# Encoder trunk in f32r halves: raw output weights also in uncomputed columns of the result, pairs in chunks 1 to 5, sums of y in chunk 0

## The chip, the cores and the metric

The kernel runs on one core of a Trainium2 chip. The metric is the device time of one execution in microseconds, as a median of three runs.

## The reference

One layer of an encoder over 256 tokens of width 4096, in float32. The stream is normalised, one input projection feeds a gated short convolution (2048 channels) and windowed attention (16 heads), both gated; their outputs, concatenated to y, pass through one output projection and a second layer norm:

```python
h = layer_norm(x, emb_ln_g, emb_ln_b)
p = h @ w_in                                    # 256 x 4096 times 4096 x 13312
y_conv = c_b * centred_short_conv(c_c * c_h, conv_w) * silu(c_z)
y_attn = banded_window_attention(a_q, a_k, a_v, sink) * silu(a_z)
y = concatenate([y_conv, y_attn]) @ w_out       # 256 x 4096 times 4096 x 4096
out = layer_norm(2 ** 0.25 * h + y, ln_g, ln_b)
```

## The kernel before

**Halves.** Each f32 operand is split into a hi part (rounded to f32r) and a lo part (the rest), and each product is three matmuls: hi x hi, hi x lo, lo x hi (L210 to L212 and L841 to L843). The weights come as raw f32 from memory. ACT copies them to `whi` (`split_hi`, L170), DVE subtracts to get `wlo` (`split_lo`, L174); three buffers of each. `xT` holds both halves of the left operand for all 32 k-tiles, first of h, later of y.

**Steps.** All weight work is one list of steps. A whole step ("s") is four k-tiles of 512 output columns, 128x2048 raw values, 1 MB, 24 matmuls of 512 columns. A pair ("S") is two k-tiles by a scheme of Strassen's kind (`mm_pair`): seven products of half size instead of eight, 21 matmuls of 256 columns, 0.5 MB raw. For a pair DVE first makes three further sums of its raw blocks (`sums`, L154 to L156, below called the adds), and the left operand has sums and differences of its own, kept in the tile `SC` (`x_sums`). `pair_copy` and `pair_sums` put the products together at the end of a chunk.

**The output projection** goes over nine chunks of output columns: seven of 512 (0 to 6) and two of 256 (7, 8). `OUT_ORDERS` gives each chunk's steps. The result collects in `R` (128 x 2 x 4096: two row tiles), chunk by chunk from column 0 on. A chunk's end (`end_out`) adds the accumulators to R and takes the statistics (L860), `end_out2` multiplies by ln_g (L864). The residual of a chunk (`res_load`) is five transfers of 256 KB each: rows of the two embedding parameters and of ln_g, broadcast to all partitions, into `gb`, and x into `xc`; `residual` (L823, L825) makes alpha times h from them. `gb` and `xc` have one buffer each. `finish_...` make the second norm at the end; `rows_load` and `rows_split` bring ln_g and ln_b to it in 15 small transfers.

**Order.** It is written by hand: at step j PE gets the matmuls of j, ACT the hi copy of j+3, then come what is due by `at`, the loads, DVE's adds of step j+4 and its lo subtraction of j+3. Each engine and SP's queue work in that order. A raw load goes to the buffer that was used longest ago: with three buffers (w0 to w2), the load of j+6 waits for the lo subtraction of j+3.

```python
while nxt < len(steps) and nxt <= j + 7:
    (u, _), bs = w_bufs(nxt)
    if u > j + (2 if len(bs) > N_W else 3):
        break
```

N_IN is the first step of the output projection. `open_p2` opens the pool of R, gb, xc and the tiles of the end at step N_IN+5, in memory that the convolution's tiles held.

Of the kernel before, what the change touches and what calls it, by code (L numbers as in the profile page):

```python
# [8 lines left out]
F32 = mybir.dt.float32  # L9
# [35 lines left out]
ORDERS = {0: "s" * 8, NP: "sSsSSsSsSSs"}  # L45
OUT = 100
OP = 4
OUT_ORDERS = ["s" * 8, "ssSsSsSsSs"] + ["sSsSssSsSs"] * 5 + ["", ""]
N_W = 3


# [43 lines left out]
def encoder_kernel(ctx: ExitStack, tc: tile.TileContext, x, emb_g, emb_b, wi, ws, conv_w, sink, wo, ln_g, ln_b, out):  # L95
# [43 lines left out]
    def loads(j):

# [8 lines left out]
    def sums(j):  # L149

        if j >= len(steps) or not is_pair(j):
            return
        r = raw[j].rearrange("p (b w) -> p b w", w=HW)
        nc.vector.tensor_tensor(r[:, 4:6, :], r[:, 1:3, :], r[:, 0:1, :].to_broadcast([P, 2, HW]), op=ALU.add)  # L154
        nc.vector.tensor_tensor(r[:, 6, :], r[:, 5, :], r[:, 1, :], op=ALU.add)
        nc.vector.tensor_tensor(r[:, 7, :], r[:, 6, :], r[:, 3, :], op=ALU.add)  # L156
# [432 lines left out]
    def sum_tile(ci):  # L589

        if ci >= OUT:
            return R[:, :, (ci - OUT) * W:(ci - OUT + 1) * W]
        kind = IN_ORDER[ci]
        if kind >= C_AZ:
            return pa.tile([P, 2, W], F32, name="z")
        if kind >= C_Q:
            return pa.tile([P, 2, W], F32, name="q")
        name = "ug" if kind < C_CC or C_CH <= kind < C_CZ else "tm"
        if pc is not None:
            return pc.tile([P, 2, W], F32, name=name)  # L600
# [90 lines left out]
    def at(j, fn, *a):  # L691
        later.setdefault(j, []).append((fn, a))
# [109 lines left out]
    def res_load(n):  # L802
# [202 lines left out]
```

## Time and profile before

| | us |
|---|---|
| median of three runs (1569.02 to 1569.75) | 1569.3 |
| the profiled execution | 1571.03 |
| its span | 1569.3 |

| engine | busy us | share of the span |
|---|---|---|
| PE | 1528.5 | 97% |
| PE weight loads | 1328.2 | 85% |
| DVE | 1298.2 | 83% |
| ACT | 759.7 | 48% |

The mean granted clock of TensorE is 0.991 of full speed. A share of busy time is a mean over the whole span; what stops PE in one stage is read from that stage's waits and timeline. "PE busy" counts a matmul until its modelled end, so the distance from one matmul's start to the next one's tells its cost.

### The profile page before, as it was taken

Reading aid. Unit: us, or ns where it says so; the run is one execution under the profiler, and the core shown is the slowest. Engines: PE = TensorE matmul, PEld = TensorE weight load, DVE = VectorE, ACT = ScalarE, POOL = GpSimd, SP = SyncE. Lnnn points to the kernel's source line nnn. Section 1 sums busy time; section 2 is a strip of 40 time slices with the busy share of each in tenths; the row PEclk is TensorE's granted clock in tenths of the full one; section 3 lists DMA queues with packets and bytes.
Section 4 is the critical chain, followed back from the end, with each engine's and each line's share of the span. In section 5 each row is a group of like instructions: output and inputs, shape, how many; then the busy total and the mean of one; then the engine's idle time right before and its main releaser. Section 6 shows DMA issues by size and latency. Waiting matters only on the chain.

```text
span 1569.3 us, 21272 instructions
## 1 busy us (share of the span) xinstructions
PE 1528.5 (97%) x8694; PEld 1328.2 (85%) x8694; DVE 1298.2 (83%) x1494; ACT 759.7 (48%) x642; POOL 1.3 (0%) x7
## 2 busy tenths in 40 slices
PE   7999999999999999999999999999999899899997
PEld 4888888888888888888888888888888787787896
DVE  8678789888888889888888888888887889678786
ACT  4544556556564654544444454454554334333341
POOL 0000000000000000000000000000000000000000
PEclk9999999999999999999999999999999999999998
DMA  7545554546445457555555655565557564665563
GB/s 296 210 143 197 199 203 158 189 167 209 178 181 188 158 183 256 204 200 191 210 201 183 220 187 203 192 210 203 198 194 262 178 232 166 224 209 216 205 244 128
DMA packets 65889, 312.99 MB, mean 199 GB/s; under 512 B 7968, under 2 KB 11520, under 8 KB 41728
## 3 DMA queue, kind: packets, MB, share of 16 engines
q1 hardware_dynamic: 65216, 310.06, 55.5%
q8 instruction: 68, 1.11, 0.3%
q10 hardware_dynamic: 576, 1.57, 0.3%
q14 instruction: 29, 0.24, 0.0%
HBM read 303.66 MB, written 7.86 MB: 199 GB/s over the span
## 4 chain that ended last, share of the span: by engine, by line
PE 78%; DVE 11%; DMA 5%; ACT 3%; issue 3%; SPq 1%; DVEq 0%; ACTq 0%
PE acc L210 14%; PE acc L212 14%; PE acc L211 14%; DVE wlo L174 5%; PE pacc L235 4%; PE pacc L234 4%; PE pacc L236 4%; PE acc L842 3%; DMA w<-in_ws 3%; PE acc L843 3%; PE acc L841 3%; PE acc L235 3%; PE acc L234 3%; PE acc L236 3%; ACT whi L170 2%
## 5 line engine op out<-in xcount | busy, mean ns | idle before, releaser
L170 ACT ACTIVATE whi<-w 128x2048 fp32r<-128x2048 f32 (+1 forms) x353 | 640.4, 1816 | 730.2 <-PE acc L212 288.8
L174 DVE TENSOR_TENSOR wlo<-w,whi 128x2048 fp32r<-128x2048 f32 (+1 forms) x353 | 759.5, 2161 | 163.3 <-ACT whi L170 161.4
L210 PE MATMUL acc<-whi,xT 128*128 128x512 f32 x1072 | 424.3, 396 | 0.0
L212 PE MATMUL acc<-whi,xT 128*128 128x512 f32 x1072 | 419.8, 392 | 0.0
L211 PE MATMUL acc<-wlo,xT 128*128 128x512 f32 x1072 | 417.8, 390 | 0.7 <-DVE wlo L174 0.7
L212 PEld LDWEIGHTS acc<-whi,xT 128*128 128x128 f32 x1072 | 201.3, 188 | 46.8
L211 PEld LDWEIGHTS acc<-wlo,xT 128*128 128x128 f32 x1072 | 201.4, 188 | 41.2 <-DVE wlo L174 1.0
L210 PEld LDWEIGHTS acc<-whi,xT 128*128 128x128 f32 x1072 | 201.5, 188 | 37.9
L842 PE MATMUL acc<-wlo,xT 128*128 128x512 f32 (+1 forms) x464 | 172.5, 372 | 18.8 <-DVE wlo L174 18.8
L843 PE MATMUL acc<-whi,xT 128*128 128x512 f32 (+1 forms) x464 | 172.3, 371 | 0.0
L841 PE MATMUL acc<-whi,xT 128*128 128x512 f32 (+1 forms) x464 | 171.5, 370 | 0.0
L154 DVE TENSOR_TENSOR w<-w 128x512 f32<-128x512 f32 x168 | 114.9, 684 | 46.7 <-DMA w<-in_ws 46.6
L842 PEld LDWEIGHTS acc<-wlo,xT 128*128 128x128 f32 x464 | 88.9, 192 | 36.1 <-DVE wlo L174 21.5
L235 PE MATMUL pacc<-wlo,SC 128*128 128x256 f32 x360 | 101.4, 282 | 0.0
L841 PEld LDWEIGHTS acc<-whi,xT 128*128 128x128 f32 x464 | 89.0, 192 | 14.5 <-issue 0.4
L843 PEld LDWEIGHTS acc<-whi,xT 128*128 128x128 f32 x464 | 89.0, 192 | 14.4
L236 PE MATMUL pacc<-whi,SC 128*128 128x256 f32 x360 | 101.1, 281 | 0.0
L234 PE MATMUL pacc<-whi,SC 128*128 128x256 f32 x360 | 101.1, 281 | 0.0
L235 PE MATMUL acc<-wlo,xT 128*128 128x256 f32 x336 | 93.8, 279 | 0.0
L234 PE MATMUL acc<-whi,xT 128*128 128x256 f32 x336 | 93.7, 279 | 0.0
L236 PE MATMUL acc<-whi,xT 128*128 128x256 f32 x336 | 93.6, 279 | 0.0
L234 PE MATMUL pacc<-whi,xT 128*128 128x256 f32 x312 | 89.1, 286 | 0.0
(205 smaller groups left out, 1812.7 us busy)
## 6 DMA issues: line engine op xcount, KB each, us to landing
w<-in_wi SPq DMA_DIRECT2D x134, 1024.0 KB
w<-in_ws SPq DMA_DIRECT2D x168, 512.0 KB
w<-in_wo SPq DMA_DIRECT2D x52, 1024.0 KB
yl<-yd SPq DMA_DIRECT2D x7, 512.0 KB
xc<-in_x SPq DMA_DIRECT2D x14, 256.0 KB
x<-in_x SPq DMA_DIRECT2D x6, 512.0 KB
first<-in_wi SPq DMA_DIRECT2D x2, 1024.0 KB
yd<-zT SPq DMA_DIRECT2D x16, 128.0 KB
```

The source lines that it names most:

```text
L154: nc.vector.tensor_tensor(r[:, 4:6, :], r[:, 1:3, :], r[:, 0:1, :].to_broadcast([P, 2, HW]), op=ALU.add)
L170: nc.scalar.activation(part(j, wh[j]), part(j, raw[j]), AF.Copy)
L174: nc.vector.tensor_tensor(part(j, wl[j]), part(j, raw.pop(j)), part(j, wh[j]).bitcast(F32), op=ALU.subtract)
L210: nc.tensor.matmul(a, xh, hk, start=(first and k == 0), stop=False)
L211: nc.tensor.matmul(a, xh, lk, start=False, stop=False)
L212: nc.tensor.matmul(a, xl, hk, start=False, stop=(last and k == PK - 1))
L234: nc.tensor.matmul(o, ah, hi[:, w, :], start=(opens and p == 0), stop=False)
L235: nc.tensor.matmul(o, ah, lo[:, w, :], start=False, stop=False)
L236: nc.tensor.matmul(o, al, hi[:, w, :], start=False, stop=(closes and last))
L841: nc.tensor.matmul(o, yh, hk, start=first, stop=False)
L842: nc.tensor.matmul(o, yh, lk, start=False, stop=False)
L843: nc.tensor.matmul(o, yl, hk, start=False, stop=last)
```

## The change

It has four parts. (1) While chunks 0 to 6 run, raw weights are also loaded into columns of R that are not computed yet: from step N_IN+6 on into R0 and R1 (columns 2048 to 4095 of the two row tiles, one raw buffer each, until the chunk that writes them nears its end), then into R2 (columns 3072 to 4095 of both row tiles, one buffer), so that there are five, then four buffers; with more than three, a load waits for a lo subtraction that already stands ahead of it in the order. (2) The pairs are in chunks 1 to 5 (four each); chunk 6 has whole steps, as chunk 0. (3) The sums of y, `x_sums` for four pairs, run at the steps 1, 2, 4 and 5 of the projection instead of 6, 8, 9 and 10; their tile takes over the memory of the input projection's SC, so it need not wait for the pool of R. (4) `end_out2` and the next `res_load` move from the end of a chunk to step 0 of the next, behind its lo subtraction; the residual is made at step 4 of a chunk. Tiles that shared R's last columns move, and t5 shrinks to 72 columns to make room.

```diff
-OUT_ORDERS = ["s" * 8, "ssSsSsSsSs"] + ["sSsSssSsSs"] * 5 + ["", ""]
+OUT_ORDERS = ["s" * 8] + ["sSsSsSsSss"] * 5 + ["s" * 8, "", ""]
...
+    in_R = [(steps.index(("opair", OUT + 4, OP - 1)) + 1, "R0"), (steps.index(("opair", OUT + 4, OP - 1)) + 1, "R1"),
+            (steps.index(("out", OUT + 6, NPC - 1)), "R2")]
 
     def w_bufs(j):
 
         bs = [(wpool, f"w{k}") for k in range(N_W)] + (extra if j < N_IN else [])
-        return min((user.get(b, -1), k) for k, b in enumerate(bs)), bs
+        if j >= N_IN and R is not None:
+            late = j > in_R[0][0]
+            bs += [(None, name) for last, name in in_R if j <= last and late == (name == "R2")]
+        last_user = lambda b: max(u for c, u in user.items() if c == b or b[1] == "R2" and c[0] is None) if (
+            b in user or b[1] == "R2") else -1
+        return min((last_user(b), k) for k, b in enumerate(bs)), bs
...
-            to = raw[j] = pool.tile([P, PIECE], F32, name=name, bufs=1)
-        if is_pair(j):
+            if pool is None:
+                to = raw[j] = {"R0": R[:, 0, D // 2:D], "R1": R[:, 1, D // 2:D], "R2": R[:, :, 3 * D // 4:D]}[name]
+            else:
+                to = raw[j] = pool.tile([P, PIECE], F32, name=name, bufs=1)
...
-    psc = phs.enter_context(tc.tile_pool(name="psc", bufs=1))
+    psc = ctx.enter_context(tc.tile_pool(name="psc", bufs=1))
     SC = psc.tile([P, NP, 2, 3, HT], F32R, name="SC")
-    extra.append((psc, "w6"))
+    pw = phs.enter_context(tc.tile_pool(name="pw", bufs=1))
+    extra.append((pw, "w6"))
...
+    def y_sums(k):
+        nonlocal SC
+        if k == 0:
+            t = psc.tile([P, NP * 2 * 3, HT], F32R, name="SCy", tag="SC")
+            SC = t[:, 0:OP * 8, :].rearrange("p (k h s) t -> p k h s t", k=OP, h=2)
+        x_sums(k, pc.tile([P, 4 * S], F32, name="xs", tag="tm"))
+
     for k in range(OP):
-        at(N_IN + (6, 8, 9, 10)[k], lambda k: x_sums(k, R[:, 1, D - 4 * S:D]), k)
+        at(N_IN + (1, 2, 4, 5)[k], y_sums, k)
+    ends = []
...
-            if t == (0 if n == ncs - 1 else 2 if not np_ and n else (7, 5, 4)[min(n, 2)]):
+            if t == 0 and n:
+                for a in ends:
+                    end_out2(*a)
+                ends = []
+                if n < ncs - 1:
+                    res_load(n)
+            if t == (0 if n == ncs - 1 else 2 if n == ncs - 2 else 4 if n else 7):
                 residual(n)
...
         if n < ncs - 1:
-            for i in range(2):
-                end_out2(n, i, end_out(n, i))
-            if n + 1 < ncs - 1:
-                res_load(n + 1)
+            ends = [(n, i, end_out(n, i)) for i in range(2)]
```

Three places where the rows show it. On SP's queue around the end of chunk 1 (w0 to w2 are the raw buffers; `in_ws` holds pairs, `in_wo` whole steps; gb and xc are the residual's loads), before:

```order
L135 DMA w2_10624<-in_ws 128x1024
L137 DMA w0_10655<-in_wo 128x2048
L137 DMA w1_10691<-in_wo 128x2048
L813 DMA gb_10704<-in_emb_g_row 128x512
L814 DMA gb_10704<-in_emb_b_row 128x512
L815 DMA gb_10704<-in_ln_g 128x512
L817 DMA xc_10705<-in_x 128x512 x2
L135 DMA w2_10739<-in_ws 128x1024
L137 DMA w0_10768<-in_wo 128x2048
```

and now (R is a raw buffer in the result's tile):

```order
L151 DMA R_10285<-in_ws 128x1024
L153 DMA R_10285<-in_wo 128x2048
L151 DMA w1_10664<-in_ws 128x1024
L153 DMA w2_10694<-in_wo 128x2048
L151 DMA w0_10733<-in_ws 128x1024
L841 DMA gb_10739<-in_emb_g_row 128x512
L842 DMA gb_10739<-in_emb_b_row 128x512
L843 DMA gb_10739<-in_ln_g 128x512
L845 DMA xc_10740<-in_x 128x512 x2
L153 DMA R_10285<-in_wo 128x2048 x2
```

Ahead of the residual's loads the queue now holds the pair and the whole step that came behind them; two whole steps into R come behind them.

On DVE at the end of chunk 0 and the start of chunk 1, before (L859 and L860 are `end_out`, L864 the products with ln_g, L578 to L446 a piece of the sums of y, L154 to L156 the adds of a pair):

```order
L859 SCALAR_TENSOR_TENSOR R_10249<-xc_10262,acc_10034 128x512
L860 BN_STATS s20_10250<-R_10249 128x6
L864 TENSOR_TENSOR R_10249<-R_10249,gb_10261 128x512
L859 SCALAR_TENSOR_TENSOR R_10249<-xc_10262,acc_10038 128x512
L860 BN_STATS s21_10251<-R_10249 128x6
L864 TENSOR_TENSOR R_10249<-R_10249,gb_10261 128x512
L578 TENSOR_TENSOR R_10249<-xT_86 128x512
L583 TENSOR_TENSOR R_10249<-R_10249 128x128 x4
L446 TENSOR_TENSOR SC_10253<-R_10249,SC_10253 128x512
L154 TENSOR_TENSOR w2_10305<-w2_10305 128x512
L155 TENSOR_TENSOR w2_10305<-w2_10305 128x256
L156 TENSOR_TENSOR w2_10305<-w2_10305 128x256
```

and now (L887 and L888 are `end_out`, L201 the lo subtraction, L892 the products, L178 to L180 the adds):

```order
L887 SCALAR_TENSOR_TENSOR R_10285<-xc_10297,acc_10037 128x512
L888 BN_STATS s20_10286<-R_10285 128x6
L887 SCALAR_TENSOR_TENSOR R_10285<-xc_10297,acc_10041 128x512
L888 BN_STATS s21_10287<-R_10285 128x6
L201 TENSOR_TENSOR wlo_10411<-R_10285,whi_10407 128x1792
L892 TENSOR_TENSOR R_10285<-R_10285,gb_10296 128x512 x2
L178 TENSOR_TENSOR w1_10336<-w1_10336 128x512
L179 TENSOR_TENSOR w1_10336<-w1_10336 128x256
L180 TENSOR_TENSOR w1_10336<-w1_10336 128x256
L201 TENSOR_TENSOR wlo_10451<-R_10285,whi_10445 128x2048
```

The products stand behind the lo subtraction of the step three ahead, and the sums of y are gone from here.

They stand on DVE in chunk 0, at its steps 4 and 5. Before (L174 lo subtraction, L686 the lo half of y, L781 and L783 the memsets of t5):

```order
L174 TENSOR_TENSOR wlo_10181<-w2_10069,whi_10173 128x2048
L686 TENSOR_TENSOR xT_86<-yl_10101,xT_86 128x4x256
L174 TENSOR_TENSOR wlo_10214<-w0_10103,whi_10207 128x2048
L686 TENSOR_TENSOR xT_86<-t0_9467,xT_86 128x2x256
L686 TENSOR_TENSOR xT_86<-t1_9468,xT_86 128x2x256
L781 MEMSET t5_10255 128x256
L783 MEMSET t5_10255 128x2x2 x3
L174 TENSOR_TENSOR wlo_10270<-w1_10145,whi_10240 128x2048
```

and now (L607 to L475 are a piece of the sums of y, L715 the lo half of y):

```order
L201 TENSOR_TENSOR wlo_10201<-w2_10072,whi_10193 128x2048
L715 TENSOR_TENSOR xT_86<-yl_10104,xT_86 128x4x256
L607 TENSOR_TENSOR xs_10232<-xT_86 128x512
L612 TENSOR_TENSOR xs_10232<-xs_10232 128x128 x4
L475 TENSOR_TENSOR SCy_10106<-xs_10232,SCy_10106 128x512
L201 TENSOR_TENSOR wlo_10242<-w0_10115,whi_10227 128x2048
L715 TENSOR_TENSOR xT_86<-t0_9470,xT_86 128x2x256
L715 TENSOR_TENSOR xT_86<-t1_9471,xT_86 128x2x256
L607 TENSOR_TENSOR xs_10272<-xT_86 128x512
L612 TENSOR_TENSOR xs_10272<-xs_10272 128x128 x4
L475 TENSOR_TENSOR SCy_10106<-xs_10272,SCy_10106 128x512
```

Each piece comes ahead of the lo subtraction of its step.

## Rows read from the trace of the kernel before

**Rows 1.** The waits between engines from 1150 us to the end (who waited <- for whom: us in total, times, longest us).

```profile
DVE w L154 <- DMA w<-in_ws: 44.3, 15, 8.8
...
PE acc L842 <- DVE wlo L174: 18.8, 7, 5.2
```

**Rows 2.** The timeline of PE in the output projection: its matmuls that stood idle before they began (start us, duration us, engine, line, operation, [idle us before <- releaser]). These eight are all of them from the first to the last output matmul.

```profile
1240.26 0.58 PE L842 MATMUL acc<-wlo,xT 128*128 128x512 f32 x1 [3.92 <-DVE wlo L174]
...
1252.01 0.50 PE L842 MATMUL acc<-wlo,xT 128*128 128x512 f32 x1 [1.94 <-DVE wlo L174]
...
1297.32 0.51 PE L842 MATMUL acc<-wlo,xT 128*128 128x512 f32 x1 [2.19 <-DVE wlo L174]
...
1347.27 0.80 PE L842 MATMUL acc<-wlo,xT 128*128 128x512 f32 x1 [5.24 <-DVE wlo L174]
...
1394.95 0.50 PE L842 MATMUL acc<-wlo,xT 128*128 128x512 f32 x1 [1.83 <-DVE wlo L174]
...
1440.53 0.51 PE L842 MATMUL acc<-wlo,xT 128*128 128x512 f32 x1 [2.46 <-DVE wlo L174]
...
1486.43 0.51 PE L842 MATMUL acc<-wlo,xT 128*128 128x512 f32 x1 [1.17 <-DVE wlo L174]
...
1538.74 0.38 PE L842 MATMUL acc<-w,xT 128*128 128x256 f32 x1 [0.77 <-DVE w L174]
```

**Rows 3.** Stretches of the span (us from its start: length; busy us and count of PE, PEld, DVE, ACT, POOL; granted TensorE clock as a share of full speed; busy share of the DMA engines; GB/s). The first is the whole projection, the others are the stretches just behind four of the gaps.

```profile
1178.00:1555.00 377.00, 357.48 (x1961) 308.30 (x1959) 295.54 (x338) 147.62 (x95) 0.00 (x0) 0.98 0.58 206
1240.00:1244.00 4.00, 3.75 (x9) 2.97 (x10) 3.23 (x8) 2.11 (x2) 0.00 (x0) 0.57 0.48 164
1298.00:1302.00 4.00, 4.00 (x13) 3.10 (x11) 2.62 (x4) 0.73 (x1) 0.00 (x0) 0.57 0.72 262
1346.00:1354.00 8.00, 6.73 (x17) 5.31 (x18) 6.59 (x6) 2.68 (x2) 0.00 (x0) 0.57 0.54 197
1440.00:1446.00 6.00, 5.47 (x17) 4.33 (x18) 4.71 (x6) 1.94 (x2) 0.00 (x0) 0.72 0.64 232
```

**Rows 4.** The chain that ended last, in order of time, around the end of chunk 1 (start us, us, what).

```profile
1283.21 0.33 SPq L813
...
1285.55 7.81 DMA w<-in_ws
...
1293.45 0.70 DVE w L154
...
1294.98 2.30 DVE wlo L174
...
1297.32 0.51 PE acc L842
```

**Rows 5.** The same chain at the ends of chunks 2 and 5: the load behind the residual's loads.

```profile
1333.93 9.38 DMA w<-in_ws
...
1475.99 6.48 DMA w<-in_ws
```

**Rows 6.** The timeline of PE around one whole step of four k-tiles and one pair (start us, duration us): the first matmul of the step, of the pair, and of the pair behind it. The same two sorts of step stand in the projection.

```profile
1143.22 0.40 PE L210 MATMUL acc<-whi,xT 128*128 128x512 f32 x1
...
1148.73 0.28 PE L234 MATMUL pacc<-whi,xT 128*128 128x256 f32 x1
...
1151.20 0.28 PE L234 MATMUL pacc<-whi,xT 128*128 128x256 f32 x1
```

**Rows 7.** The timeline of DVE in chunk 1 (start us, us, engine, line, operation, count, [idle before <- releaser]). The length of a piece of work is the start of the next row's work less its own start.

```profile
1240.12 0.68 DVE L578 TENSOR_TENSOR R<-xT 128x512 f32<-128x512 f32 x1
...
1243.16 2.02 DVE L174 TENSOR_TENSOR wlo<-w,whi 128x1792 fp32r<-128x1792 f32 x1
...
1261.31 0.74 DVE L823 SCALAR_TENSOR_TENSOR xc<-xc,musd,gb 128x512 f32<-128x512 f32 x1
...
1264.21 2.29 DVE L174 TENSOR_TENSOR wlo<-w,whi 128x2048 fp32r<-128x2048 f32 x1
...
1272.30 0.41 DVE L614 TENSOR_TENSOR R<-R,pacc 128x256 f32<-128x256 f32 x1
...
1275.27 0.69 DVE L154 TENSOR_TENSOR w<-w 128x512 f32<-128x512 f32 x1
...
1276.79 2.28 DVE L174 TENSOR_TENSOR wlo<-w,whi 128x2048 fp32r<-128x2048 f32 x1
1278.99 0.68 DVE L857 TENSOR_TENSOR R<-acc,R 128x512 f32<-128x512 f32 x1
...
1283.11 4.22 DVE L174 TENSOR_TENSOR wlo<-w,whi 128x1792 fp32r<-128x1792 f32 x2
```

**Rows 8.** ACT's hi copies in the projection, by shape (xcount | busy us, mean ns | idle before, releasers): 128x2048 for a whole step, 128x1792 for a pair.

```profile
L170 ACT ACTIVATE whi<-w 128x2048 fp32r<-128x2048 f32 x49 | 93.9, 1915 | 109.3 <-PE acc L843 78.0 <-issue 11.6 <-PE pacc L236 8.6
L170 ACT ACTIVATE whi<-w 128x1792 fp32r<-128x1792 f32 x24 | 40.9, 1702 | 92.9 <-PE acc L843 48.6 <-DVE w L156 36.6 <-PE pacc L236 4.2
```

**Rows 9.** The timeline of DVE in chunk 0: the lo subtractions for the steps 7 and 8 from the start of the projection, each of which began when ACT's hi copy was done.

```profile
1208.12 2.29 DVE L174 TENSOR_TENSOR wlo<-w,whi 128x2048 fp32r<-128x2048 f32 x1 [2.06 <-ACT whi L170]
...
1213.66 2.29 DVE L174 TENSOR_TENSOR wlo<-w,whi 128x2048 fp32r<-128x2048 f32 x1 [1.50 <-ACT whi L170]
```

**Rows 10.** The stretch from the first of chunk 2's residual loads to the landing of the pair's load behind them (columns as in rows 3).

```profile
1283.20:1293.40 10.20, 10.20 (x57) 8.80 (x56) 4.12 (x2) 2.18 (x2) 0.00 (x0) 1.00 0.83 256
```

**Rows 11.** The timeline of SP's queue: the 15 small transfers of `rows_split` in chunk 2 (start us, us until the last was issued).

```profile
1319.16 11.55 SPq L800 DMA_DIRECT2D rows<-R  x15
```

More of the change, by code (lines that the diff above doesn't have):

```diff
@@ L117, in encoder_kernel @@
     raw, wh, wl = {}, {}, {}
-    psc = pc = None
+    psc = pw = pc = R = None
     extra = []
     user = {}
+    in_R = [(steps.index(("opair", OUT + 4, OP - 1)) + 1, "R0"), (steps.index(("opair", OUT + 4, OP - 1)) + 1, "R1"),
+            (steps.index(("out", OUT + 6, NPC - 1)), "R2")]
     def w_bufs(j):
         bs = [(wpool, f"w{k}") for k in range(N_W)] + (extra if j < N_IN else [])
-        return min((user.get(b, -1), k) for k, b in enumerate(bs)), bs
+        if j >= N_IN and R is not None:
[4 more added lines that the diff above has]
+        return min((last_user(b), k) for k, b in enumerate(bs)), bs
     def load(j, to=None):
@@ L132, in load @@
             user[bs[k]] = j
-            to = raw[j] = pool.tile([P, PIECE], F32, name=name, bufs=1)
-        if is_pair(j):
+            if pool is None:
+                to = raw[j] = {"R0": R[:, 0, D // 2:D], "R1": R[:, 1, D // 2:D], "R2": R[:, :, 3 * D // 4:D]}[name]
+            else:
+                to = raw[j] = pool.tile([P, PIECE], F32, name=name, bufs=1)
+        src = wi[IN_PIECES.index((a, b))] if kind == "in" else wo[OUT_PIECES.index((a, b))] if kind == "out" else None
+        if len(to.shape) == 3:
+            if is_pair(j):
+                nc.sync.dma_start(out=to[:, 0, :], in_=ws[ALL_PAIRS.index((a, b))])
+            else:
+                nc.sync.dma_start(out=to, in_=src.rearrange("p (i n) -> p i n", i=2))
+        elif is_pair(j):
             nc.sync.dma_start(out=to[:, 0:4 * HW], in_=ws[ALL_PAIRS.index((a, b))])
         else:
-            nc.sync.dma_start(out=to, in_=wi[IN_PIECES.index((a, b))] if kind == "in" else wo[OUT_PIECES.index((a, b))])
+            nc.sync.dma_start(out=to, in_=src)
     def loads(j):
@@ L152, in sums @@
             return
[L153 to L156, printed above, removed]
+        if len(raw[j].shape) == 3:
+            r0, r1 = (raw[j][:, i, :].rearrange("p (b w) -> p b w", w=HW) for i in range(2))
+            r = lambda k: (r1 if k >= 4 else r0)[:, k % 4, :]
+            s01 = r1[:, 0:2, :]
+            b12, b22 = r0[:, 0:1, :], r0[:, 1:3, :]
+        else:
+            t = raw[j].rearrange("p (b w) -> p b w", w=HW)
+            r = lambda k: t[:, k, :]
+            s01, b12, b22 = t[:, 4:6, :], t[:, 0:1, :], t[:, 1:3, :]
+        nc.vector.tensor_tensor(s01, b22, b12.to_broadcast([P, 2, HW]), op=ALU.add)
+        nc.vector.tensor_tensor(r(6), r(5), r(1), op=ALU.add)
+        nc.vector.tensor_tensor(r(7), r(6), r(3), op=ALU.add)
     def part(j, t):
+        if len(raw[j].shape) == 3:
+            return t if len(t.shape) == 3 else t.rearrange("p (i n) -> p i n", i=2)
         return t[:, HW:] if is_pair(j) else t
@@ L173, in split_lo @@
         wl[j] = half_tile(j, "wlo")
-        nc.vector.tensor_tensor(part(j, wl[j]), part(j, raw.pop(j)), part(j, wh[j]).bitcast(F32), op=ALU.subtract)
+        nc.vector.tensor_tensor(part(j, wl[j]), part(j, raw[j]), part(j, wh[j]).bitcast(F32), op=ALU.subtract)
+        raw.pop(j)
     def split(j):
@@ L601, in sum_tile @@
         if name == "tm":
-            st_["cu"] = psc.tile([P, 2, 2, W], F32, name="w6", bufs=1)
+            st_["cu"] = pw.tile([P, 2, 2, W], F32, name="w6", bufs=1)
         return st_["cu"][:, 1 if name == "ug" else 0, :, :]
@@ L737, in encoder_kernel @@
         if j == z0 + 6:
-            extra.insert(0, (psc, "w6"))
+            extra.insert(0, (pw, "w6"))
         mm_pair(j) if kind == "pair" else mm(j)
@@ L761, in encoder_kernel @@
     res = {}
-    p2 = R = st2 = ms2 = rows = t5 = lhs5 = None
+    p2 = st2 = ms2 = rows = t5 = lhs5 = None
     RB = [(0, 0), (0, 1), (0, 2), (32, 0), (32, 1), (32, 2), (64, 0), (64, 1)]
@@ L770, in open_p2 @@
     def open_p2():
-        nonlocal p2, R, st2, ms2, rows, t5, lhs5, SC
+        nonlocal p2, R, st2, ms2, rows, t5, lhs5
         ph.close()
@@ L777, in open_p2 @@
         ms2 = p2.tile([P, 2, 4], F32, name="ms2")
-        SC = p2.tile([P, OP, 2, 4, HT], F32R, name="SC")
         rows = p2.tile([P, 3 * W], F32R, name="rows")
-        t5 = p2.tile([P, 2, P], F32, name="t5")
+        t5 = p2.tile([P, 2, 72], F32, name="t5")
         nc.vector.memset(t5, 0.0)
@@ L789, in rows_load @@
         for k, src in enumerate((ln_g, ln_b)):
-            w = lnw[k] = R[0:KT, k, D - 4 * P:D - 3 * P]
+            w = lnw[k] = R[0:KT, k, 3 * W:3 * W + P]
             nc.sync.dma_start(out=w, in_=src.rearrange("(a b) -> a b", b=P))
@@ L794, in rows_split @@
         for k, (slots_h, slot_l) in enumerate((((0, 1), 2), ((3,), 4))):
-            w, hl = lnw[k], R[0:KT, k, D - 3 * P:D - P].bitcast(F32R).rearrange("p (a b) -> p a b", a=2)
+            w, hl = lnw[k], R[0:KT, k, 3 * W + P:3 * W + 3 * P].bitcast(F32R).rearrange("p (a b) -> p a b", a=2)
             nc.vector.tensor_copy(hl[:, 0, :], w)
@@ L809, in res_load @@
         else:
-            z = p2.tile([P, OP * 2 * 4, HT], F32, name="z", tag="SC").rearrange("p a b -> p (a b)")
+            z = psc.tile([P, NP * 2 * 3, HT], F32, name="z", tag="SC").rearrange("p a b -> p (a b)")
             gb = z[:, 0:3 * w].rearrange("p (a b) -> p a b", a=3)
@@ L881, in finish_tr @@
         tp = ps_att.tile([P, P], F32, name="att")
-        nc.tensor.transpose(tp, t5[:, i, :], ident)
+        nc.tensor.transpose(tp[0:72, :], t5[:, i, :], ident)
         nc.scalar.activation(lhs5[0:69, i, :], tp[0:69, :], AF.Copy)
```

## The prediction

> **What bounds the kernel now.** I read the page first, then the waits of the last quarter, PE's timeline there, the granted clock, the chain and DVE's timeline. The change touches nothing ahead of the output projection, so only its 377 us count. The page has PE busy for 97% of the span, and in the projection it is busy for 357.5 of 377 us [rows 3]: the bound is PE, with gaps. The gaps are eight, each in front of the second matmul of a step, which needs the step's lo half from DVE: 3.92 + 1.94 + 2.19 + 5.24 + 1.83 + 2.46 + 1.17 + 0.77 = 19.5 us [rows 2]. Behind the gaps of 3.92, 2.19, 5.24 and 2.46 us the granted clock stands at its lower level (1.2 instead of 2.4 GHz) for some us. The loss is the share below 1 times the length: 0.43 x 4 + 0.43 x 4 + 0.43 x 8 + 0.28 x 6 = 8.6 us [rows 3]; the whole projection's 0.98 of 377 us says that little is lost elsewhere. After the gaps of 1.94, 1.83 and 1.17 us it stayed high. Gaps and clock together: 28.1 us.
>
> Why is DVE late? It waited 44.3 us for pair loads [rows 1], and since it works in order, a pair's adds that wait for their load hold up the lo subtraction queued behind them, which PE needs sooner. The worst loads stand behind the residual's five loads, at a chunk's end. There the chain goes: products with ln_g done, first residual load issued at 1283.21, the pair's load issued at 1285.55 and landed 7.81 us later, adds at 1293.45, lo at 1294.98, PE at 1297.32 [rows 4]. At other chunk ends that load took 9.38 and 6.48 us [rows 5].
>
> **The parts of the change, with t for a step of a chunk and E(t) for the time PE ends it.** A whole step takes PE 5.51 us, a pair 2.47 [rows 6].
>
> *Pairs in five chunks.* Four pairs (9.9 us) become two whole steps (11.0): +1.1 us of PE time, on the path.
>
> *Raw buffers in R.* With three buffers a load waited for the lo subtraction three steps ahead of it; with five (chunks 1 to 4) it waits for the one five steps ahead, with four (chunk 5) four. In a paired chunk two steps are 8.0 us, about what the late pair loads took. SP's rows show it: seven steps are loaded ahead of the residual's loads instead of six, and no pair load follows them in these chunks. Bytes are the same (four loads of half a MB for two of one), and the DMA engines were busy for 0.58 of the stage [rows 3].
>
> Does DVE then keep up? Work per paired chunk [rows 7]: six whole lo at 2.2 (1276.79 to 1278.99), four pair lo at 2.0, four adds at 1.5 [rows 4], 3.0 for the pairs' sums with the residual (1272.30 to 1275.27), 2.9 for the residual (1261.31 to 1264.21), 4.1 for the chunk's end (1278.99 to 1283.11): 37.3 us of PE's 42.9. Counted from E(0): E(1) 2.5, E(2) 8.0, E(3) 10.5, E(4) 16.0, E(5) 18.4, E(6) 23.9, E(7) 26.4. A hi copy starts when PE has freed its buffer and takes 1.9 us, for a pair 1.7 [rows 8]. So lo(3) ends at 3.7, the moved products at 5.1, adds(5) at 6.6, lo(4) at 8.8, due at 10.5. Later hi(7) ends at 17.7, lo(7) at 19.7, the residual at 22.6, lo(8) at 24.8, due at 26.4. The margin is 1.6 us at both places and larger elsewhere: no gap in chunks 2 to 4. The old end-of-chunk gaps go; what is late next is the pair load in chunk 5. Its four buffers leave the pair of t = 7 behind the residual's loads: products at 5.1, plus 10.2 us from first residual issue to adds [rows 4], is 15.3, where lo(5) ended at 11.7. Adds to 16.8, lo(6) to 19.0, due at 18.4: +0.6 us.
>
> The DVE and ACT operations that read R have no row; their shapes are those of the w buffers, so I take the same durations. Bounds: nothing either way, since where R is an operand a row is no slower (0.68 us for 128x512 at 1240.12 [rows 7], 0.70 for the same size in w [rows 4]).
>
> `rows_split` in chunk 2 still puts 15 small transfers on SP, 11.6 us [rows 11]. Two raw loads stand behind them; counting on from the chunk's end they land some 11 to 13 us into chunk 3, wanted at 10.5 to 11.7 with 2 us to spare before PE notices: 0, at most 3.
>
> *Products and residual loads one step later.* The two products (a third of 4.1, 1.4 us) leave the chunk's end and go behind lo(3). At the very end this also puts the last lo ahead of them, so the 0.77 us gap goes. Queued behind the moved loads on SP are the loads for t = 8 and 9, wanted 10 us after.
>
> *Sums of y in chunk 0.* Four pieces of 3.0 us each (1240.12 to 1243.16) leave chunks 0 and 1, where they made the gaps of 3.92 and 1.94 us, for t = 1, 2, 4 and 5 of chunk 0. There DVE waited 2.06 and 1.50 us for ACT ahead of lo(7) and lo(8) [rows 9], so the first three cost only DVE's spare time. In the old run lo(7) began at 1208.12 and lo(8) at 1213.66, with 1.8 us of other work between. Now the sums at t = 4 make lo(7) end at about 1212.8 (1208.1, three ACT copies and one DVE subtraction of together 2.5, then 2.2), the last sums end at 1217.3, adds(9) at 1219, lo(8) at 1221.2. PE ended step 5 at 1213.66 - 1.92 = 1211.7, so it ends step 7 at 1222.7: 1.5 us to spare.
>
> *What is late next: the start of chunk 1.* R can be used only once the last sums of y are done, because its pool opens then, and SP puts chunk 0's residual loads ahead of the first R load. Issue at 1217.3 plus 10.2 gives 1227.5 for the pair of step 11. DVE, idle from 1223, then has adds(11) to 1229.0 and lo(10) to 1231.2, due at 1230.7: 0.5 late. Residual 2.9 and chunk end without products 2.7: 1236.9. lo(11) to 1238.9, due at 1236.7: 2.2 late. Products 1.4, adds(13) 1.5, lo(12) 2.2: 1244.0, due at 1241.4: 2.6 late. Together 5.3 us of gaps, and one spell at the lower clock, 1.7 us, as after the gaps of 2.19 and 2.46: 7.0 us. If the load lands 4 us sooner nearly all of it goes; if 3 us later, and with two spells, it is 12.
>
> Here a rule of the Trainium skill bears (DMA: Bandwidth & Descriptors, Queues, rings and completion order): each DMA engine takes the descriptors of one queue in ring order, so loads issued behind the pair's would not delay it. The trace does not quite agree: until that pair landed 10.2 us x 256 GB/s = 2.6 MB had moved [rows 10], 0.8 MB more than residual and pair hold, so some of the later load went too. By the rule the 10.2 us stand and the sum is 1550; by sharing, the half MB more behind the pair now adds 2 us and the sum is 1552.
>
> *The sum.* 1569.3 - 28.1 + 1.1 + 7.0 + 0.6 = 1549.9 us of span. The profiled execution took 1571.03 us with a span of 1569.3, so 1.7 us lie around the span; the median of the runs shown is 1569.3, that much lower than the profiled one. I carry the difference of -19.4 us to the median: **1550 us**.
>
> **The rivals.** *All gaps close.* The first R load lands by 1223, for instance because the residual's loads find the engines empty. For it: a DMA share of only 0.58; against: four chunk ends with nearly the same landing. 1569.3 - 28.1 + 1.1 = 1542.3.
>
> *DVE becomes the bound.* The margins of 1.6 us are small against 37.3 of 42.9 us of work, and a pair's adds still stand ahead of a nearer lo. If each of the chunks 1 to 5 keeps a gap of 2 us, which the clock survives by rows 2, that is 10 us: 1560. For it: DVE was busy most where PE stood still; against: its longest waits were for DMA, not for work.
>
> *It does not do what it says.* The residual's loads still block SP until the products are done, and if that wait rather than the buffers set the landings, the gaps at chunk ends stay and only the 0.77 us, the two of chunk 1 in part and one spell go: about 1567.
>
> *Slower.* The place is t = 8 of chunks 1 to 5: two loads of one MB into R directly behind the residual's 1.3 MB, 3.4 MB in one batch issued from 5.1. PE needs them landed by 22.3. At 256 GB/s [rows 10] they are there at 18.4; at the 164 GB/s of a quiet stretch [rows 3] at 25.8, and ACT, in order, holds every later hi copy. The gap is then 3.5 us and a spell of 1.7 in each of five chunks, 26 us: 1576. It decides from about 170 GB/s downward.
>
> **How the numbers follow.** Forecast 0.50, all gaps close 0.18, DVE the bound 0.20, no effect 0.07, slower 0.05. The first three are faster by more than 0.2% (3.1 us, about what a measurement of this kernel can tell from no change): 0.88. No effect falls within it, mostly: 0.06; slower 0.06. The range reaches from the second case to just past the third: 1542 to 1562.
>
> **What would show it.** In the profile after: sums of y in t = 1, 2, 4, 5 of chunk 0 and no gap at PE there; gaps of PE between about 1230 and 1244, some 5 us in all, with one spell at the lower clock; nothing above 1 us at the ends of chunks 1 to 4; DVE's wait for pair loads down from 44.3 us to below 15, the longest at the first R load. Wrong would be gaps at every chunk (then see whether DVE is full or waits for R's loads), or step 8 late in chunk 0, or a lower clock without a gap.

## The result and the profile after

Four runs of the changed kernel gave a median of 1552.28 us (1551.15 to 1553.11), four of the kernel before 1569.53 us: a ratio of 0.9888, with a 95% interval of 0.9871 to 0.9906. The profiled execution took 1551.15 us, its span 1549.2 us, 20.1 us less than before. What is given per step below is read from that execution.

The windows of the changed kernel: the whole projection, then the stretch around the start of chunk 1 (columns: length, busy us of each engine, granted clock, DMA share, GB/s).

```profile
1178.00:1535.00 357.00, 354.04 (x1925) 304.87 (x1923) 282.20 (x318) 144.98 (x92) 0.00 (x0) 1.00 0.61 217
1230.00:1236.00 6.00, 5.67 (x28) 4.52 (x27) 5.86 (x9) 2.65 (x2) 0.00 (x0) 1.00 0.51 194
1236.00:1242.00 6.00, 4.20 (x25) 3.81 (x24) 5.93 (x8) 0.49 (x1) 0.00 (x0) 0.82 0.15 30
1242.00:1248.00 6.00, 5.17 (x22) 3.91 (x22) 5.93 (x6) 3.02 (x2) 0.00 (x0) 0.89 0.87 273
1248.00:1254.00 6.00, 6.00 (x39) 5.35 (x38) 4.20 (x4) 3.63 (x2) 0.00 (x0) 1.00 1.00 423
```

The projection is 20 us shorter with nearly the same busy time of PE [rows 3]. One spell at the lower clock is left of four: 0.18 x 6 + 0.11 x 6 = 1.74 us, where before lost 8.6.

PE's timeline, the rows with a gap in front (in brackets its length and what ended it). These are all above 0.25 us before the tail:

```profile
1231.21 0.51 PE L870 MATMUL acc<-wlo,xT 128*128 128x512 f32 x1 [0.33 <-DVE wlo L201]
...
1238.67 0.39 PE L263 MATMUL pacc<-wlo,xT 128*128 128x256 f32 x1 [1.80 <-DVE wlo L201]
...
1243.60 0.50 PE L870 MATMUL acc<-wlo,xT 128*128 128x512 f32 x1 [0.83 <-DVE wlo L201]
```

Three gaps, 2.96 us, all at the start of chunk 1, stand against eight and 19.5 us [rows 2]. The gap at the very end (0.77) is gone too. The waits from 1150 us on show the same from DVE's side: the 44.3 us for pair loads [rows 1] have become 4.3 + 3.0.

```profile
ACT whi L197 <- DMA R<-in_wo: 4.4, 2, 3.8
DVE R L178 <- DMA R<-in_ws: 4.3, 1, 4.3
...
DVE w L178 <- DMA w<-in_ws: 3.0, 1, 3.0
...
PE pacc L263 <- DVE wlo L201: 1.8, 1, 1.8
...
PE acc L870 <- DVE wlo L201: 1.2, 2, 0.8
```

The 4.3 us are the first pair in R. SP's queue and DVE's timeline show where it stood: first residual load out at 1217.02, the pair's at 1219.29, its adds (L178) at 1227.34, and everything behind them late.

```profile
1217.02 0.33 SPq L841 DMA_DIRECT2D gb<-in_emb_g_row  x1
...
1219.29 0.72 SPq L151 DMA_DIRECT2D R<-in_ws  x1
```

```profile
1216.25 0.69 DVE L475 TENSOR_TENSOR SCy<-xs,SCy 128x512 fp32r<-128x512 f32 x1 [0.70 <-ACT SCy L474]
...
1218.81 4.22 DVE L201 TENSOR_TENSOR wlo<-w,whi 128x2048 fp32r<-128x2048 f32 x2
1227.34 0.69 DVE L178 TENSOR_TENSOR R<-R 128x512 f32<-128x512 f32 x1 [4.30 <-DMA R<-in_ws]
...
1228.87 2.29 DVE L201 TENSOR_TENSOR wlo<-w,whi 128x2048 fp32r<-128x2048 f32 x1
...
1236.61 2.01 DVE L201 TENSOR_TENSOR wlo<-R,whi 128x1792 fp32r<-128x1792 f32 x1
1238.53 1.28 DVE L892 TENSOR_TENSOR R<-R,gb 128x512 f32<-128x512 f32 x2
1239.74 0.69 DVE L178 TENSOR_TENSOR w<-w 128x512 f32<-128x512 f32 x1
...
1241.26 2.28 DVE L201 TENSOR_TENSOR wlo<-R,whi 128x2048 fp32r<-128x2048 f32 x1
```

One loss was not there before: the pitch, the time from one matmul's start to the next one's, is longer in some steps. The starts of PE's matmuls around the start of chunk 2: the first of a whole step (24 matmuls) and of what comes behind it, for the last step of chunk 1 and for t = 2 of chunk 2:

```profile
1265.00 0.40 PE L869 MATMUL acc<-whi,xT 128*128 128x512 f32 x1
...
1270.60 0.40 PE L869 MATMUL acc<-whi,xT 128*128 128x512 f32 x1
...
1278.68 0.40 PE L869 MATMUL acc<-whi,xT 128*128 128x512 f32 x1
...
1284.18 0.28 PE L262 MATMUL pacc<-whi,xT 128*128 128x256 f32 x1
```

The first whole step takes 5.60 us, the second 5.50, with the granted clock at 1.00 and no wait in either. Counted over chunks 1 to 5, 16 whole steps have the slower pitch, 233 ns a matmul instead of 229, some 1.6 us in all; in before no step of the projection that runs without a gap has it.

### The profile page after: what moved, and what is told of

Read it like the earlier page. It is cut to its first block, busy times and chain, and to the rows that moved or that the text cites. A ratio compares the mean times of both kernels' runs of the same rounds, so it can differ in the third digit from the quotient of the medians.

```text
span 1549.2 us, 21154 instructions
## 1 busy us (share of the span) xinstructions
PE 1525.1 (98%) x8658; PEld 1325.1 (86%) x8658; DVE 1285.0 (83%) x1474; ACT 756.9 (49%) x639; POOL 1.3 (0%) x7
## 4 chain that ended last, share of the span: by engine, by line
PE 88%; DVE 5%; ACT 2%; issue 2%; DMA 2%; DVEq 0%; SPq 0%; ACTq 0%
PE acc L238 15%; PE acc L240 14%; PE acc L239 14%; PE acc L870 6%; PE acc L869 6%; PE acc L871 6%; PE pacc L263 4%; PE pacc L262 4%; PE pacc L264 4%; PE acc L263 3%; PE acc L262 3%; PE acc L264 3%; DVE wlo L201 2%; ACT whi L197 1%; DMA x<-in_x 1%
## 5 line engine op out<-in xcount | busy, mean ns | idle before, releaser
L197 ACT ACTIVATE whi<-w 128x2048 fp32r<-128x2048 f32 (+1 forms) x332 | 602.4, 1815 | 680.3 <-PE acc L240 288.9
L201 DVE TENSOR_TENSOR wlo<-w,whi 128x2048 fp32r<-128x2048 f32 (+1 forms) x332 | 715.0, 2160 | 188.0 <-ACT whi L197 186.2
L870 PE MATMUL acc<-wlo,xT 128*128 128x512 f32 (+1 forms) x480 | 176.1, 367 | 1.2 <-DVE wlo L201 1.2
L869 PE MATMUL acc<-whi,xT 128*128 128x512 f32 (+1 forms) x480 | 176.8, 368 | 0.0
L871 PE MATMUL acc<-whi,xT 128*128 128x512 f32 (+1 forms) x480 | 176.3, 367 | 0.0
L178 DVE TENSOR_TENSOR w<-w 128x512 f32<-128x512 f32 x160 | 109.4, 683 | 5.0 <-DMA w<-in_ws 4.9
L264 PE MATMUL acc<-whi,xT 128*128 128x256 f32 x328 | 91.6, 279 | 0.0
L262 PE MATMUL acc<-whi,xT 128*128 128x256 f32 x328 | 91.5, 279 | 0.0
L262 PE MATMUL pacc<-whi,xT 128*128 128x256 f32 x308 | 88.0, 286 | 0.0
L263 PE MATMUL pacc<-wlo,xT 128*128 128x256 f32 x308 | 86.1, 280 | 1.8 <-DVE wlo L201 1.8
L264 PE MATMUL pacc<-whi,xT 128*128 128x256 f32 x308 | 85.8, 279 | 0.0
L263 PE MATMUL pacc<-wlo,SC 128*128 128x256 f32 x288 | 81.0, 281 | 0.0
```

Source lines behind the costliest of these rows:

```text
L178: nc.vector.tensor_tensor(s01, b22, b12.to_broadcast([P, 2, HW]), op=ALU.add)
L197: nc.scalar.activation(part(j, wh[j]), part(j, raw[j]), AF.Copy)
L201: nc.vector.tensor_tensor(part(j, wl[j]), part(j, raw[j]), part(j, wh[j]).bitcast(F32), op=ALU.subtract)
L262: nc.tensor.matmul(o, ah, hi[:, w, :], start=(opens and p == 0), stop=False)
L263: nc.tensor.matmul(o, ah, lo[:, w, :], start=False, stop=False)
L264: nc.tensor.matmul(o, al, hi[:, w, :], start=False, stop=(closes and last))
```

## The experiments

My theory (T1): loads into R run far enough ahead that the residual's five loads no longer stand between a pair and its adds. Rivals: the later products and residual loads did it (T2), the moved sums of y did it (T3). Each ratio is to the kernel before, timed on the same chip. Gaps are PE's above 0.25 us in the projection, clock is what spells at the lower clock lost there, by the six-us windows. e9, e10 and e11 ran on another chip than the rest of the table; the kernel before took 1570.96 us there, 0.5 less than beside the others.

| kernel | median us | ratio, 95% interval | gaps us | clock us |
|---|---|---|---|---|
| changed, again | 1551.31 | 0.9869 (0.9853 to 0.9885) | 3.9 | 1.7 |
| e1, three buffers | 1563.31 | 0.9952 (0.9937 to 0.9967) | 12.8 | 3.4 |
| e6, four buffers | 1560.13 | 0.9930 (0.9915 to 0.9944) | 10.6 | 1.7 |
| e2, products at the end | 1557.53 | 0.9909 (0.9895 to 0.9924) | 8.6 | 3.4 |
| e3, sums late | 1554.31 | 0.9890 (0.9874 to 0.9907) | 6.4 | 3.4 |
| e10, e2 and e3 | 1560.86 | 0.9938 (0.9925 to 0.9952) | 10.4 | 5.2 |
| e5, order of before | 1549.66 | 0.9862 (0.9847 to 0.9877) | 2.3 | 0 |
| e4, pair load first | 1547.30 | 0.9846 (0.9832 to 0.9861) | 1.1 | 0 |
| e8, e4, products later | 1545.68 | 0.9837 (0.9823 to 0.9852) | 0 | 0 |
| e9, e8 in before's order | 1544.83 | 0.9835 (0.9821 to 0.9848) | 0 | 0 |
| e11, e9 with six chunks | 1543.28 | 0.9824 (0.9811 to 0.9838) | 0 | 0 |

**e1: no raw weights in R.**

```diff
-        if j >= N_IN and R is not None:
+        if False:
```

> Raw weights stay in the three w buffers; order of the pairs, moved products and residual loads, and early sums of y stay as in the changed kernel. If the deeper buffering is what took the gaps away (my reading), the residual's five loads again stand ahead of a pair load that is wanted soon: a gap of about 2 us or more in most of the chunks 1 to 5, some with a spell at the lower clock, and DVE's wait for pair loads back above 25 us: 1560 to 1572 us. If the later products and residual loads did it (rival), the time stays at 1550 to 1555 us and DVE waits for pair loads under 15 us.

1563.31 us, 12.0 above the changed kernel's 1551.31 (before stood at 1571.6 and 1571.5 beside them). DVE's waits for pair loads:

```profile
DVE w L178 <- DMA w<-in_ws: 34.3, 10, 5.2
```

As T1 had it: seven gaps, in all of the chunks 1 to 5. T2 alone is out.

**e6: one raw buffer in R instead of two.**

```diff
-    in_R = [(steps.index(("opair", OUT + 4, OP - 1)) + 1, "R0"), (steps.index(("opair", OUT + 4, OP - 1)) + 1, "R1"),
+    in_R = [(steps.index(("opair", OUT + 4, OP - 1)) + 1, "R0"),
```

> One raw buffer in R instead of two in chunks 1 to 4 (four in all, as chunk 5 has them in the changed kernel); all else as in the changed kernel. If each buffer more moves one load ahead of the residual's: the pair of t = 7 stands behind the residual's loads in each chunk, DVE waits about 3 us for it, PE has gaps of 0 to 0.6 us as in chunk 5: 1552 to 1557 us, most of the 12 us between three buffers and five. If only five do: near the 1563 us of three buffers.

1560.13 us: the step that was to be late is, but costs far more than I took from chunk 5. In chunk 1 the pair of t = 7 goes out behind the residual's loads, at 1242.24, and DVE waits longer than there:

```profile
1249.87 0.69 DVE L178 TENSOR_TENSOR R<-R 128x512 f32<-128x512 f32 x1 [4.32 <-DMA R<-in_ws]
```

Of the 12 us between three and five buffers the fifth gives 8.8. It is the one that puts the last pair of a chunk ahead of the residual's loads; the fourth alone does not.

**e2: products and residual loads back at the chunk's end.**

```diff
-            if t == 0 and n:
-                for a in ends:
-                    end_out2(*a)
-                ends = []
-                if n < ncs - 1:
-                    res_load(n)
...
-            ends = [(n, i, end_out(n, i)) for i in range(2)]
+            for i in range(2):
+                end_out2(n, i, end_out(n, i))
+            if n + 1 < ncs - 1:
+                res_load(n + 1)
```

> Products with ln_g and the residual's loads go back to the end of a chunk; the five buffers stay. If buffering is the cause: within 2 us of the changed kernel (1550 to 1555), plus the 0.8 us gap ahead of the last step, and no gap above 1 us at the chunk ends. If the rival holds, SP stands behind the products again and the gaps at the chunk ends come back: 1560 us or more.

1557.53 us, between the two. Chunks 2 and 4 have no gap, as T1 had it, but chunk 3 has one of 3.87 us at t = 6, which neither had. SP's queue and DVE's timeline ahead of it:

```profile
1313.29 11.61 SPq L828 DMA_DIRECT2D rows<-R  x15
1325.00 0.38 SPq L153 DMA_DIRECT2D w<-in_wo  x1
1325.49 0.37 SPq L841 DMA_DIRECT2D gb<-in_emb_g_row  x1
...
1328.14 0.53 SPq L151 DMA_DIRECT2D w<-in_ws  x1
```

```profile
1337.86 0.69 DVE L178 TENSOR_TENSOR w<-w 128x512 f32<-128x512 f32 x1 [6.84 <-DMA w<-in_ws]
```

and PE's gap:

```profile
1341.72 0.56 PE L870 MATMUL acc<-wlo,xT 128*128 128x512 f32 x1 [3.87 <-DVE wlo L201]
```

The 15 small transfers of `rows_split` delay the queue; with the residual's loads then ahead of the pair of t = 7, DVE waits 6.84 us for it. In the changed kernel that pair goes first and the delay costs nothing; its SP queue at the same place:

```profile
1313.46 11.63 SPq L828 DMA_DIRECT2D rows<-R  x15
1325.19 0.38 SPq L153 DMA_DIRECT2D w<-in_wo  x1
1325.68 0.37 SPq L151 DMA_DIRECT2D w<-in_ws  x1
1326.14 0.38 SPq L841 DMA_DIRECT2D gb<-in_emb_g_row  x1
```

So part 4 is worth 6.2 us; the gap of 3.87 and the spell behind it (0.28 x 6 = 1.7) are 5.6 of them. A gap of 0.73 at t = 6 of chunk 5 and the 0.77 at the very end are there too.

**e3: sums of y at steps 6, 8, 9 and 10 again**, in columns 1024 to 2047 of R, which hold no raw weights.

```diff
-        x_sums(k, pc.tile([P, 4 * S], F32, name="xs", tag="tm"))
+        x_sums(k, R[:, 1, D // 2 - 4 * S:D // 2])
...
-        at(N_IN + (1, 2, 4, 5)[k], y_sums, k)
+        at(N_IN + (6, 8, 9, 10)[k], y_sums, k)
```

> Sums of y back at steps 6, 8, 9 and 10, in columns of R that hold no raw weights; all else as in the changed kernel. R then opens some 6 us sooner, so the first pair load into R goes out near 1211 instead of 1219. If the sums belong in chunk 0's spare time: DVE has their 12 us again while the first pairs come, a gap of 3 to 4 us near 1236 and a spell at the lower clock, 1554 to 1560 us. If the earlier opening of R makes up for it: 1550 to 1553 us, with gaps under 3 us.

1554.31 us (1552.93 to 1555.08), 3.0 above the changed kernel's 1551.31, just inside the first expectation. R opens sooner and DVE waits only 0.7 us for the first pair in it, but then two of the sums stand ahead of lo subtractions:

```profile
1237.19 0.38 PE L263 MATMUL pacc<-wlo,xT 128*128 128x256 f32 x1 [1.25 <-DVE wlo L201]
...
1245.16 0.79 PE L870 MATMUL acc<-wlo,xT 128*128 128x512 f32 x1 [5.12 <-DVE wlo L201]
```

Early sums delay R, late ones fill DVE; the first is the cheaper.

**e10: e2 and e3 together**, so that the buffers and the pairs' chunks stand alone.

> The five buffers and the pairs in five chunks alone: products and residual loads at the chunk's end as in e2, sums of y at steps 6, 8, 9 and 10 as in e3. If the parts add up: 1551.5 plus some 6 us (e2) plus some 2.5 us (e3), 1560 us. If they hide each other (the residual loads go out before R is wanted, DVE has the products done before the first pair): 1556 to 1558 us.

1560.86 us: the parts add up (6.2 + 3.0 = 9.2; measured 9.5, or 10.1 with the 0.5 us between the chips). Of the change's gain of some 20 us (1571.46 to 1551.31 in one set of runs), buffers and chunks alone give half (1570.96 to 1560.86), parts 3 and 4 the other half; without the fifth buffer (e6, with parts 3 and 4) 8.8 are lost too.

**e5: the order of steps of before** in chunks 1 to 5.

```diff
-OUT_ORDERS = ["s" * 8] + ["sSsSsSsSss"] * 5 + ["s" * 8, "", ""]
+OUT_ORDERS = ["s" * 8] + ["sSsSssSsSs"] * 5 + ["s" * 8, "", ""]
```

> Chunks 1 to 5 in before's order of steps (sSsSssSsSs) instead of sSsSsSsSss; all else as in the changed kernel. The last pair is then the last step but one, so the pairs' sums with the residual (3.0 us) stand at the chunk's end next to its 2.7 us. If the order is part of the gain: gaps of 1 to 2 us at the chunk ends, 1556 to 1562 us. If the buffers alone keep the loads early: within 2 us of 1552.

1549.66 us: no gap at any chunk's end. The new order is no part of the gain. If anything it costs: here no whole step that runs without a wait has the slow pitch, though the times of the two kernels overlap (1547.88 to 1551.92 here).

**The changed kernel again**, without an edit.

> The changed kernel once more, unedited. In its first profile the whole steps t = 0, 4, 8 and 9 of chunks 2 to 5 ran at 233 ns per matmul and the others at 229, and the 256-wide matmuls of the last two chunks at 119 ns, where before had 113; no wait is shown. If the program sets the pitch: the same steps are slow again, and the time is within 1 us of 1552. If the history of one execution sets it: other steps are slow, and the spread of the times is some 2 us.

The same 16 whole steps are slow, and the last chunks too: the program sets the pitch, not the one execution. The times are 1550.04 to 1552.32. PE's gaps differ a little:

```profile
1238.41 0.38 PE L263 MATMUL pacc<-wlo,xT 128*128 128x256 f32 x1 [1.80 <-DVE wlo L201]
...
1243.34 0.50 PE L870 MATMUL acc<-wlo,xT 128*128 128x512 f32 x1 [2.08 <-DVE wlo L201]
```

**e4: the first pair load into R ahead of chunk 0's residual loads.**

```diff
                 open_p2()
+                loads(j)
                 res_load(0)
             loads(j)
```

> The first two loads into R (the pair of step 11 and step 12) go out on SP ahead of the residual's five loads of chunk 0; nothing else moves. If the late landing of that pair, at 1227.3, is the whole cause of the three gaps (2.96 us) and of the spell at the lower clock (1.7 us): it lands by 1224, DVE does not wait for it, the gaps go and the time falls by 3 to 5 us to about 1548. If the residual's loads were not in its way (the DMA engines share among all that is issued): the pair lands within 1.5 us of 1227 and the time stays within 1.5 us of 1552.

1547.30 us, 4.0 below. The load goes out at 1216.58, and DVE takes the pair up without waiting:

```profile
1222.51 0.68 DVE L178 TENSOR_TENSOR R<-R 128x512 f32<-128x512 f32 x1
...
1234.48 1.28 DVE L892 TENSOR_TENSOR R<-R,gb 128x512 f32<-128x512 f32 x2
1235.68 0.69 DVE L178 TENSOR_TENSOR w<-w 128x512 f32<-128x512 f32 x1
...
1237.21 2.28 DVE L201 TENSOR_TENSOR wlo<-R,whi 128x2048 fp32r<-128x2048 f32 x1
```

The late landing was the cause of two of the three gaps and of the spell. The third stayed, at 1.12 us and 1239.54, as the lo that PE waits for stands behind the two products.

**e8: e4, and chunk 0's products with chunk 1's residual loads one step later.**

```diff
-            if t == 0 and n:
+            if t == (1 if n == 1 else 0) and n:
```

> The pair load ahead of the residual's loads as in e4, and chunk 0's two products and chunk 1's residual loads one step later (t = 1 of chunk 1 instead of t = 0). In e4 one gap is left, 1.12 us at 1239.5, ahead of a lo that stands behind the two products (1.28 us). If DVE's order is its cause: the gap goes, no gap above 0.3 us is left in the projection, and the time is 1.1 us under e4, or more by a pitch that falls well. If something else sets that lo (its hi copy, its load): the gap stays at about 1.1 us.

1545.68 us (1544.71 to 1547.62; e4 had 1546.49 to 1548.26, so the times overlap). In the trace PE is busy without a break, so DVE's order was the cause of that gap:

```profile
1178.00:1528.00 350.00, 350.00 (x1919) 301.93 (x1918) 281.35 (x317) 144.86 (x92) 0.00 (x0) 1.00 0.61 221
```

**e9: e8 with the order of e5.**

> e8 with chunks 1 to 5 in before's order of steps (sSsSssSsSs). In the profile of e5 no whole step ran at 233 ns per matmul, and in before but one, so the order may set that pitch. If it does: no whole step above 230 ns in the chunks 1 to 6, no gap, and the time is about 1.5 us under e8. If e5 was fast because its gaps of 1.8 and 0.5 us happened to fall well: slow steps here too, and the time of e8 within 1 us.

1544.83 us (1544.48 to 1545.63), on the other chip. That is 0.85 below e8, of which 0.5 may be the chip, and the ratios to before (0.9835 and 0.9837) do not tell the two apart; a gain of the 1.5 us that were expected is not shown. The traces show more. No whole step of the chunks 1 to 6 is slow; one from its start to what follows:

```profile
1265.31 0.40 PE L869 MATMUL acc<-whi,xT 128*128 128x512 f32 x1
...
1270.80 0.28 PE L262 MATMUL pacc<-whi,xT 128*128 128x256 f32 x1
```

5.49 us. The last two chunks begin at 1480.88, 1.5 us sooner than in e8 (1482.37), but part of that is lost again there: the 256-wide matmuls of the last two chunks run at the slower pitch in e9 and at the faster for most of them in e8.

**e11: e9 with pairs in chunk 6 too**, 24 in all; the buffer in the last quarter of R then ends with that chunk's last pair.

```diff
-OUT_ORDERS = ["s" * 8] + ["sSsSssSsSs"] * 5 + ["s" * 8, "", ""]
+OUT_ORDERS = ["s" * 8] + ["sSsSssSsSs"] * 6 + ["", ""]
...
-            (steps.index(("out", OUT + 6, NPC - 1)), "R2")]
+            (steps.index(("opair", OUT + 6, OP - 1)) + 1, "R2")]
```

> e9 with pairs in chunk 6 too (24 pairs as in before, in six chunks); the raw buffer in the last quarter of R serves chunk 6 up to its last pair. If four buffers are enough in chunk 6: two whole steps (11.0 us) become four pairs (9.9 us), no gap, 1.1 us under e9. If not: pair loads late by 1 to 3 us in chunk 6, the time equal to e9 or up to 3 us above.

1543.28 us (1542.91 to 1543.83), 1.55 below e9 and without a gap: faster than both kernels, 1.8% under before. DVE waits for a pair 4.3 us at the longest, and PE for nothing.

## Why the prediction was right, and where it was not

The time forecast was 1550, the range 1542 to 1562; it came to 1552.3, with the span at 1549.2 where 1549.9 was worked out. Step by step:

*Gaps and clock of before, 28.1 us:* gone, as forecast, and e1 brings much of them back. But the step "seven steps are loaded ahead of the residual's loads instead of six, and no pair load follows them" was put down to the buffers alone, and there it failed: with five buffers and the old place of the residual's loads (e2) the pair of t = 7 again follows them, harmless in chunks 2 and 4, 5.6 us with `rows_split` ahead of it. I had priced part 4 by its products and by the 0.77 us at the end; its worth is the order of SP's queue. `rows_split` itself cost 0, as taken, but only in that order.

*Pairs in five chunks, +1.1:* e11 takes it back, and measures 1.55 against e9 on the same chip.

*Chunk 0:* right. The last sums of y end at 1216.9 (forecast 1217.3), and no gap follows at t = 5 to 7.

*Start of chunk 1:* right in mechanism, and nearly to the row: adds at 1227.34 (1227.5), the lo behind it ends at 1231.2 (1231.2), the chunk's end at 1236.7 (1236.9), lo(12) at 1243.5 (1244.0). Gaps 0.33 + 1.80 + 0.83, forecast 0.5 + 2.2 + 2.6, and one spell, 1.74 against 1.7. The third term was mis-sized mainly because I added gap and spell as if they were apart: the pair at t = 3 took from 1236.6 to 1242.1, 5.5 us, with a part of it at the lower clock. In the second profile the spell came behind the third gap: there the same pair took 4.5 us (1236.33 to 1240.86), and the third gap is 2.08 instead of 0.83. DVE caught up in the time that the lower clock cost PE. That there was one spell is in part luck: e5 has a gap of 1.81 us at the same place and none. e4 shows the cause of the first two gaps and of the spell: with the load first, they go.

*Ring order or sharing:* adds 10.3 us after the first residual load (1217.02 to 1227.34), as 10.2 had been taken; sharing would have added 2. The Trainium skill's rule (DMA: Bandwidth & Descriptors, Queues, rings and completion order) fits this landing. The trace's DMA packets show it too: the residual's packets (2 KB) move from 1217.98 on, the pair's (4 KB) only from 1223.33, though the pair was issued at 1219.29. The order is not strict: before the pair's last packet began, at 1226.78, 80 packets of 8 KB (0.66 MB) of the step behind it had begun, of the size of the 0.8 MB that the prediction found too much. In e4 the pair, sent first, is there at most 5.9 us after its issue (1216.58 to 1222.51), where it took 8.0 behind the residual's loads.

*Chunks 2 to 4, margins of 1.6 us:* no gap, as forecast; e5 has none either, with the pairs' sums at the chunk's end.

*Chunk 5, 0.6:* DVE waited 3.0 us there, and PE lost 0.25: the step at t = 6 took 5.75 us (1424.56 to 1430.31) instead of 5.50, with no idle row long enough for the list above. e6 shows how little that says: four buffers in every chunk cost 8.8 us.

*No term at all:* the slower pitch. 16 whole steps times 0.10 = 1.6 us, and in the last two chunks 21 matmuls take 2.47 us (from 1490.21 on) where before took 2.38 (from 1507.77) up to its gap at 1538.74; over these 30 us that is 1.1 us more. Together 2.7 us. The sum with it: 1569.3 - 28.1 + 1.1 + (2.96 + 1.74) + 0.25 + 2.7 = 1549.95, measured 1549.2. The rest of 0.8 fits that a gap cost PE somewhat more than its idle time, which the 28.1 left out: before's step from 1484.87 to 1491.82 took 6.95 us, 0.29 more than 5.49 and its gap of 1.17. The 7.6 us that I had for the start of chunk 1 and for chunk 5 were 4.95, and the 2.7 missing ones came from elsewhere: that 1549.9 was so close is in part luck.

*The rivals:* "All gaps close" needed two more edits, those of e4 and e8: it is e8, without a gap and with a span of 1542.8 us, where 1542.3 was worked out. DVE was not the bound: it was busy for 282.2 of 357 us, and in the chunks 2 to 4 PE has no gap. "It does not do what it says" had a true half: SP's order of residual and pair loads decides (e2, e4). "Slower" fell: the hi copies waited 4.4 us for whole steps in R, and PE for none of them.

## What to carry to other kernels

More buffers help only by what they let pass: count which load stands behind which in the queue, for each buffer more; the fourth here gave 3 us, the fifth 9. When a late load is found, look first whether a load that is wanted later stands ahead of it: moving two loads past five cost nothing and gave 4 us. And a gap and a spell at the lower clock behind it are not to be added blindly, since a slower PE gives the late engine time.

## What the runs showed of the hardware

Matmuls without any wait, at a granted clock of 1.00, have two start-to-start times: 229 or 233 ns at 512 columns, and in the last two chunks 113 or 118 ns at 256. Which one holds changes at pairs and where PE was held up, if only for 0.1 us (in e3 at 1521.44). With the steps in before's order (before, e5, e9, e11) no whole step of the chunks 1 to 6 that runs without a wait is slow; with the changed kernel's order some are, and which ones depends on what went ahead: t = 0, 4, 8 and 9 in the changed kernel and in e3 (chunks 2 to 4), t = 2 and 6 in e4. In the last two chunks e2, e3, e8 and e10 begin at 113 ns, as before does; the changed kernel, e1, e4, e5, e6, e9 and e11 begin at 118. The Trainium skill (TensorE: Matmul & The Clock Gate, Back-to-back issue gap) gives one isolated gap of N / 2.4 + 2.5 ns, 216 ns at 512, and about 131 ns in a sustained stream; the traces here, with 229 and 233, agree with neither. What sets the pitch stays open: no run changed it alone.

The length of a gap does not decide alone whether the lower clock follows. The gap of 1.80 us at t = 3 of chunk 1 had a spell right behind it in the first profile of the changed kernel (granted clock 0.82 from 1236 to 1242 and 0.89 from 1242 to 1248). In the second profile the same gap of 1.80 had none until the next gap of 2.08 was over (1.00 from 1236 to 1242), and in e5 1.81 us had none at all. So the prediction's order of lengths, 1.94 us survived and 2.19 not, held for the one execution that it was read from.
